# All three terms of a split float32 product summed in the same 256 PSUM columns, with another weight offset in each layer

## The chip, the cores and the metric

The kernel runs on one core of a Trainium2 chip. The metric is device time in microseconds (us) of one execution. Before the change it is 2197.75 us, the median of three runs (2196.8 to 2198.79).

## What is computed

The reference is a two-layer decoder trunk on 256 tokens of width 2048, in float32. Cut to what matters:

```python
for layer in range(2):
    hn = rms_norm(h, mix_norm_w[layer])
    mix = even_mixer(hn, ...) if layer % 2 == 0 else odd_mixer(hn, ...)
    h = h + mix
    f = conv_ffn(rms_norm(h, ffn_norm_w[layer]), ...)   # (silu(conv(hn @ w_gate)) * (hn @ w_up)) @ w_down
    h = h + f
return rms_norm(h, final_norm_w)
```

`even_mixer` is one wide input projection that feeds stick-breaking attention (8 heads) and a Mamba-2 state-space part, and an output projection. `odd_mixer` is dilated attention with 16 heads. The feed-forward width is 5632. Nearly all arithmetic is in the large matrix products, and all their weights are read once from device memory.

## The kernel before, in words

**Split products.** TensorE takes its operands as `float32r`. Each float32 operand is therefore kept as two parts, a rounded `hi` and the rest `lo`, and a product is the sum of three terms: w_hi·x_hi, w_hi·x_lo and w_lo·x_hi. An activation tile (`x`, `act` or `o`, 128 partitions x 512 columns) holds x_hi of the 256 tokens in its first half and x_lo in its second.

**Weights.** `prep` (L131) loads a chunk of 512 KB (128 x 1024) into a `raw` tile (4 buffers) with a DMA from SyncE's queue, ScalarE casts it into the hi part of an `hl` tile (3 buffers; L149), and VectorE subtracts to get the lo part (L150). In `hl` the hi part begins 48 elements into the tile and the lo part 1040 elements after it. In the built program every `x`, `act`, `o` and `hl` tile starts 64 bytes past a multiple of 128 bytes, so the distance from an activation tile to a weight part, taken modulo 128 bytes, is the part's offset in the tile times 4: 64 for hi, 0 for lo.

**Matmuls.** `chan` (L214) works off one chunk: weights stationary (128 x 128), tokens moving. For each of 2 output tiles and 4 slices k, a 512 wide matmul multiplies w_hi by x_hi and x_lo side by side into 512 PSUM columns, and a 256 wide one adds w_lo·x_hi to the first 256. So the sum of a product stands in two halves of a PSUM bank, and the eviction has to add them: `total` (L280) copies one half to SBUF on ScalarE (L284) and adds the other on VectorE (L285), and `project` (L376) adds both halves to the residual (L387, L388). A group of `chan` work has two PSUM banks out of the four of the `acc` pool. The opening (L161) does the first columns of the even layer with weights of its own layout: 16 tiles of `wfirst`, 816 columns each, of which `FB` = 304 belong to the first part; there six 272 wide matmuls (L186) with tokens stationary stand beside four pairs of 512 and 256 (L194, L196). `tok` (L226) does value projections with the roles turned: tokens stationary, weights moving, 512 wide (L231) and 256 wide (L238); its weights stand 48 elements into `hl` and it is not changed. `wide` (L413) does the last projections, 512 wide, L419.

**Order.** `products` (L245) walks over the chunks of a layer; background generators (attention, the state-space part, normalisation) give out a piece of their work per chunk. The engines' order is set when the program is built, by a scheduler that follows its own estimate of when operands are ready; each engine then works strictly in that order. The state-space part needs 32 rows of sums, which go to device memory (`rows`, L818, a DMA from ScalarE's queue) and come back broadcast to all partitions (`sr`, L823, four DMAs of 512 KB from GpSimd's queue). VectorE uses them at L875. Phases: even layer, feed-forward 0, odd layer, feed-forward 1.

Of the kernel before, what the change touches and what calls it, by code (L numbers as in the profile page):

```python
# [21 lines left out]
FT = FF // P  # L22
CH = 4

FB = 304
FW = FB + 2 * T
SBH = 8
SBW = 1024
# [36 lines left out]
class Trunk:  # L65
# [5 lines left out]
    def __init__(self, ctx, tc, a):  # L71
        self.tc = tc
        self.nc = tc.nc
        self.a = a
        pool = lambda name, bufs, **kw: ctx.enter_context(tc.tile_pool(name=name, bufs=bufs, **kw))
        self.cst = pool("cst", 1)
        self.hp = pool("hp", 1)
        self.xp = pool("xp", KT)
        self.wraw = pool("wraw", 4)
        self.whl = pool("whl", 3)  # L80
        self.dram = pool("dram", 1, space=bass.MemoryType.DRAM)
        self.ev = pool("ev", 3)
        self.nrm = pool("nrm", 2)
        pool("gap", 1).tile([P, 48], F32, name="gap")
        self.acc = pool("acc", 4, space=bass.MemoryType.PSUM)
        self.aux = pool("aux", 4, space=bass.MemoryType.PSUM)
        self.n = 0
        self.bg = []
        self.last = None
        self.strict = {}  # L90

    def nm(self, s):
        self.n += 1
# [37 lines left out]
    def prep(self, src, apart=False, off=48):  # L131


        nc = self.nc
        ch, ncol = src.shape[-2:]
        n = ch * ncol
        raw = self.wraw.tile([P, CH * 272], F32, tag="raw", name=self.nm("raw"))[:, :n]
        hl = self.whl.tile([P, CH * 544], F32R, tag="hl", name=self.nm("hl"))
        raw = raw.rearrange("p (c n) -> p c n", n=ncol)
        if apart:  # L140
            both = hl = tuple(
                hl[:, o : o + n].rearrange("p (c n) -> p c n", n=ncol) for o in (48, 48 + n + 16)
            )
        else:
            hl = hl[:, off : off + 2 * n].rearrange("p (c t n) -> p c t n", t=2, n=ncol)
            both = (hl[:, :, 0], hl[:, :, 1])
        nc.sync.dma_start(raw, src)
        hi, lo = both
        nc.scalar.copy(hi, raw)  # L149
        nc.vector.tensor_tensor(lo, raw, hi.bitcast(F32), ALU.subtract)  # L150
        return hl
# [9 lines left out]
    def opening(self, xs):  # L161


        nc = self.nc
        mm = nc.tensor.matmul
        accs = [self.banks(self.acc), self.banks(self.acc), self.banks(self.aux)]
        n = T + SSH
        lo0 = FW + 32
        for k in range(KT):
            raw = self.wraw.tile([P, CH * 272], F32, tag="raw", name=self.nm("raw"))  # L170
            hl = self.whl.tile([P, CH * 544], F32R, tag="hl", name=self.nm("hl"))
            parts = (slice(0, FB), slice(FB, FW)) if k == 0 else (slice(0, FW),)
            for s in parts:
                self.then(nc.sync, "dma_start", raw[:, s], self.a["wfirst"][k][:, s])
            xs.load(k + 1 + k // 4)
            for s in parts:
                hi, lo = hl[:, s], hl[:, lo0 + s.start : lo0 + s.stop]
                self.then(nc.scalar, "copy", hi, raw[:, s])
                self.then(nc.vector, "tensor_tensor", lo, raw[:, s], hi.bitcast(F32), ALU.subtract)
                if k == s.start == 0:  # L180
                    xs.split(0)
            xs.split(k + 1 + k // 4)
            x = xs[k]
            for p, w in ((0, 0), (0, lo0), (1, 0)):
                for tt in range(NT):
                    mm(  # L186
                        accs[0][tt][:, :n], x[:, p * T + tt * P : p * T + (tt + 1) * P], hl[:, w : w + n],
                        start=k == p == w == 0, stop=k == KT - 1 and p == 1,
                    )
            for j in (0, 1):  # L190
                for nt in range(2):
                    acc = accs[1 + j][nt]
                    c = FB + j * T + nt * P
                    mm(acc, hl[:, c : c + P], x, start=k == 0, stop=False)  # L194
                    c += lo0
                    mm(acc[:, :T], hl[:, c : c + P], x[:, :T], start=False, stop=k == KT - 1)  # L196
            if k == KT - 1:
                self.strict = None
            self.tick()
        return accs  # L200
# [13 lines left out]
    def chan(self, accs, hl, xs, k0, start, stop):  # L214


        for nt in range(2):
            for k in range(CH):
                for w in range(2):
                    n = (2 - w) * T  # L220
                    self.nc.tensor.matmul(  # L221
                        accs[nt][:, :n], hl[w][:, k, nt * P : (nt + 1) * P], xs[k0 + k][:, :n],
                        start=start and k == w == 0, stop=stop and w == 1 and k == CH - 1,
                    )

    def tok(self, accs, hl, xs, k0, start, stop):  # L226
# [47 lines left out]
    def tick(self):  # L274

        for g in list(self.bg):
            if next(g, self) is self:
                self.bg.remove(g)

    def total(self, acc):  # L280

        nc = self.nc
        t = self.ev.tile([P, T], F32, tag="ev", name=self.nm("ev"))
        nc.scalar.copy(t, acc[:, T:])  # L284
        nc.vector.tensor_tensor(t, acc[:, :T], t, ALU.add)  # L285
        return t

    def padded(self, n, count):

# [86 lines left out]
    def project(self, panels, xs, normw, order=None):  # L376

        nc = self.nc
        sums = []
        out = []  # L380

        def done(g):
            def f(accs):
                for nt, acc in enumerate(accs):
                    kt = 2 * g + nt
                    h = self.h[kt]
                    nc.vector.tensor_tensor(h, acc[:, T:], h, ALU.add)  # L387
                    nc.vector.tensor_tensor(h, acc[:, :T], h, ALU.add)  # L388
                    out.append(self.split_scaled(h, normw(kt)))
                self.square(sums, self.pair(2 * g))  # L390

            return f

        self.products([(self.chan, panels[g], done(g)) for g in range(KT // 2)], xs, order)
        return out, sums
# [96 lines left out]
    def ffn(self, l, xs, sums, normw, out=None):  # L492
# [10 lines left out]
        def gate(g):  # L503
            def f(accs):
                for nt, acc in enumerate(accs):
                    j = 2 * g + nt
                    gp = gpad[j % 3]
                    nc.vector.tensor_tensor(gp[:, 2:], self.total(acc), self.rbc, ALU.mult)  # L508
                    c = self.t256("cv", 4)
                    w = lambda i: self.par("fcw", (l * 3 + i) * FT + j)  # L510
                    nc.scalar.activation(c, gp[:, 2:], AF.Copy, scale=w(2))  # L511
                    nc.vector.scalar_tensor_tensor(c, gp[:, 1 : T + 1], w(1), c, ALU.mult, ALU.add)  # L512
                    nc.vector.scalar_tensor_tensor(c, gp[:, :T], w(0), c, ALU.mult, ALU.add)  # L513
                    self.last = nc.scalar.activation(c, c, AF.Silu, bias=self.par("fcb", l * FT + j))  # L514
                    nc.gpsimd.tensor_tensor(c, c, self.rbc, ALU.mult)  # L515
                    sil[j] = c

            return f

        def up(g):  # L520
            def f(accs):
                for nt, acc in enumerate(accs):
                    j = 2 * g + nt
                    u = self.total(acc)
                    nc.vector.tensor_tensor(u, u, sil.pop(j), ALU.mult)  # L525
                    self.split(u, act[j])

            return f
# [131 lines left out]
    def heads(self, panels, g, attend, o, v=None, vi=0):  # L660
# [9 lines left out]
        def qdone(accs):  # L670
            for acc in accs:
                t = self.t256("q")
                nc.vector.scalar_tensor_tensor(t, self.total(acc), ISD, self.rbc, ALU.mult, ALU.mult)
                q.append(t)

        def kdone(accs):
            for acc in accs:
                t = self.t256("k")
                nc.vector.tensor_tensor(t, self.total(acc), self.rbc, ALU.mult)
                k.append(t)  # L680
            self.bg.append(attend(q, k, v, o, vi))

# [25 lines left out]
    def even(self, xs, sums, normw):  # L708
# [21 lines left out]
        def convdone(g):  # L730

            def f(accs):
                pair = self.big("ssd", 14, F32)
                self.convs.append(pair)
                for nt, acc in enumerate(accs):
                    j = 2 * g + nt
                    cp = cpad[j % 2]
                    nc.vector.tensor_tensor(cp[:, 3:], self.total(acc), self.rbc, ALU.mult)
                    c = self.t256("cv", 3)
                    w = lambda i: self.par("ecw", i * 12 + j)  # L740
                    nc.scalar.activation(c, cp[:, 3:], AF.Copy, scale=w(3))
# [10 lines left out]
        def zdone(accs):  # L752
            pair = self.big("ssd", 14, F32)
            for nt, acc in enumerate(accs):
                c = self.total(acc)
                nc.vector.tensor_tensor(c, c, self.rbc, ALU.mult)
                dst = pair[:, nt * T : (nt + 1) * T]
                self.last = nc.scalar.activation(dst, c, AF.Silu)
                zs.append(dst)
# [152 lines left out]
    def run(self, out):  # L912
# [53 lines left out]

        xs = Input()
        ffnw = lambda l: lambda k: self.par("ffnw", l * KT + k)
        for step in (
            lambda x, s: self.even(x, s, ffnw(0)),  # L970
            lambda x, s: self.ffn(0, x, s, lambda k: self.par("mixw", KT + k)),
            lambda x, s: self.odd(x, s, ffnw(1)),
        ):
            with self.phase() as self.ph:
                xs, sums = step(xs, sums)
        with self.phase() as self.ph:
            self.ffn(1, xs, sums, None, out)


# [94 lines left out]
```

## Time and profile before

| | |
|---|---|
| median of the runs | 2197.75 us |
| the profiled execution, whole | 2196.1 us |
| its span, first to last instruction | 2194.0 us |
| TensorE busy | 2181.3 us, 12414 matmuls |
| TensorE weight loads | 1909.6 us, 12414 loads |
| VectorE busy | 1438.4 us |
| ScalarE busy | 1139.8 us |
| mean DMA rate | 190 GB/s |

In the rows of the profile PE is TensorE's matmul, PEld its weight load, DVE VectorE, ACT ScalarE, POOL GpSimd and SP SyncE. A matmul record is some 160 ns longer than the time to the next start, since matmuls are pipelined: how fast TensorE goes is read from the starts (or from the number that starts in a window), never from the mean length of a record.

### The profile page before, as it was taken

To read this page: it belongs to the slowest core of one execution; us is meant where nothing else is said; L and a number is where in the kernel's file an instruction comes from. 1 tells how busy PE (TensorE), PEld (TensorE's weight loads), DVE (VectorE), ACT (ScalarE), POOL (GpSimd) and SP (SyncE) were. 2 spreads that over 40 slices of the span, in tenths; PEclk is the share of its full clock that TensorE was granted. 3 is DMA by queue.
4 is the path that set the end of the run, shared out by engine and by line. 5 is a ranking of instruction groups with operands and counts; after the bars stand their busy time and mean duration, and the time that the engine had idled before them with its cause. 6 is when DMAs were issued, how large, how long until landed. Compare 5 with 4: busy or idle time off the path is not lost.

```text
span 2194.0 us, 32170 instructions
## 1 busy us (share of the span) xinstructions
PE 2181.3 (99%) x12414; PEld 1909.6 (87%) x12414; DVE 1438.4 (66%) x2096; ACT 1139.8 (52%) x1647; POOL 96.8 (4%) x107
## 2 busy tenths in 40 slices
PE   9999999999999999999999999999999999999998
PEld 8888888888888888888888888888888888888886
DVE  8678776766667665555566556667667676654444
ACT  7456554555555554444455454546555555554443
POOL 0000000111101010000000000000010101100000
PEclk9999999999999999999999999999999999999999
DMA  7754556666666666666655555566566666666664
GB/s 251 231 175 152 173 181 193 189 195 192 193 194 193 196 194 193 193 192 195 195 176 175 180 168 179 183 212 189 184 193 194 194 196 194 192 194 193 196 195 154
DMA packets 117129, 417.43 MB, mean 190 GB/s; under 512 B 13008, under 2 KB 15216, under 8 KB 116848
## 3 DMA queue, kind: packets, MB, share of 16 engines
q1 hardware_dynamic: 115776, 412.48, 61.0%
q8 instruction: 97, 1.59, 0.3%
q0 software_dynamic: 576, 2.10, 0.3%
q10 hardware_dynamic: 624, 0.81, 0.1%
q14 instruction: 56, 0.46, 0.1%
HBM read 413.22 MB, written 2.11 MB: 189 GB/s over the span
## 4 chain that ended last, share of the span: by engine, by line
PE 98%; DMA 1%; DVE 0%; ACT 0%; issue 0%; POOL 0%; DVEq 0%
PE acc L221 78%; PE acc L419 15%; PE acc L231 1%; PE acc L194 1%; PE acc L186 1%; DMA sr<-rows 1%; PE acc L238 1%; PE acc L196 0%; PE aux L613 0%; PE aux L644 0%; PE aux L635 0%; PE aux L890 0%; PE aux L159 0%; PE aux L552 0%; PE aux L596 0%; PE aux L645 0%
## 5 line engine op out<-in xcount | busy, mean ns | idle before, releaser
L150 DVE TENSOR_TENSOR hl<-raw,hl 128x1024 fp32r<-128x1024 f32 x764 | 935.0, 1224 | 676.2 <-ACT hl L149 669.3
L221 PE MATMUL acc<-x,hl 128*128 128x512 f32 (+1 forms) x7680 | 1320.5, 333 | 2.7 <-DVE hl L150 2.6
L221 PEld LDWEIGHTS acc<-x,hl 128*128 128x128 f32 x7680 | 1156.9, 188 | 153.9 <-DVE hl L150 4.0
L149 ACT CAST hl<-raw 128x1024 fp32r<-128x1024 f32 x764 | 802.1, 1050 | 834.6 <-PE acc L221 527.5
L419 PE MATMUL acc<-hl,act 128*128 128x512 f32 x1056 | 239.5, 389 | 0.0
L221 PE MATMUL acc<-act,hl 128*128 128x512 f32 (+1 forms) x1408 | 239.5, 332 | 0.0
L221 PEld LDWEIGHTS acc<-act,hl 128*128 128x128 f32 x1408 | 211.8, 188 | 27.6
L419 PEld LDWEIGHTS acc<-hl,act 128*128 128x128 f32 x1056 | 198.1, 188 | 41.1
L221 PE MATMUL acc<-o,hl 128*128 128x512 f32 (+1 forms) x1024 | 175.1, 333 | 0.0
L221 PEld LDWEIGHTS acc<-o,hl 128*128 128x128 f32 x1024 | 154.1, 188 | 20.1
L284 ACT COPY ev<-acc 128x256 f32<-128x256 f32 x244 | 90.6, 373 | 148.3 <-PE acc L221 146.3
L515 POOL TENSOR_TENSOR cv<-cv,rbc 128x256 f32<-128x256 f32 x88 | 93.7, 1083 | 860.3 <-ACT cv L514 860.3
L285 DVE TENSOR_TENSOR ev<-acc,ev 128x256 f32<-128x256 f32 x244 | 102.0, 420 | 5.0 <-ACT ev L284 3.1
L419 PE MATMUL acc<-hl,x 128*128 128x512 f32 x384 | 90.5, 393 | 0.0
L419 PEld LDWEIGHTS acc<-hl,x 128*128 128x128 f32 x384 | 71.5, 188 | 14.8
L525 DVE TENSOR_TENSOR ev<-ev,cv 128x256 f32<-128x256 f32 x88 | 38.3, 437 | 10.2 <-POOL cv L515 1.5
L292 POOL MEMSET pad<- 128x2 f32 (+1 forms) x8 | 0.5, 100 | 929.7 <-PE acc L221 929.7
L514 ACT ACTIVATE cv<-cv,params 128x256 f32<-128x256 f32 x88 | 40.0, 502 | 0.0
L511 ACT ACTIVATE cv<-pad,params 128x256 f32<-128x256 f32 x88 | 39.9, 504 | 0.0
L508 DVE TENSOR_TENSOR pad<-ev,rbc 128x256 f32<-128x256 f32 x88 | 37.5, 426 | 3.0
L512 DVE SCALAR_TENSOR_TENSOR cv<-pad,params,cv 128x256 f32<-128x256 f32 x88 | 38.4, 478 | 0.0
L513 DVE SCALAR_TENSOR_TENSOR cv<-pad,params,cv 128x256 f32<-128x256 f32 x88 | 38.4, 477 | 0.0
(187 smaller groups left out, 842.7 us busy)
## 6 DMA issues: line engine op xcount, KB each, us to landing
raw<-in_wg SPq DMA_DIRECT2D x176, 512.0 KB, 3.7
raw<-in_wu SPq DMA_DIRECT2D x176, 512.0 KB, 3.6
raw<-in_wd SPq DMA_DIRECT2D x176, 512.0 KB, 3.6
raw<-in_wev SPq DMA_DIRECT2D x76, 512.0 KB, 4.0
raw<-in_wod SPq DMA_DIRECT2D x64, 512.0 KB, 3.6
raw<-in_wevo SPq DMA_DIRECT2D x32, 512.0 KB, 4.1
raw<-in_wodv SPq DMA_DIRECT2D x32, 512.0 KB, 3.9
raw<-in_wodo SPq DMA_DIRECT2D x32, 512.0 KB, 3.5
```

The source lines that it names most:

```text
L149: nc.scalar.copy(hi, raw)
L150: nc.vector.tensor_tensor(lo, raw, hi.bitcast(F32), ALU.subtract)
L221: self.nc.tensor.matmul(accs[nt][:, :n], hl[w][:, k, nt * P : (nt + 1) * P], xs[k0 + k][:, :n], start=start and k == w == 0, stop=stop and ...
L284: nc.scalar.copy(t, acc[:, T:])
L285: nc.vector.tensor_tensor(t, acc[:, :T], t, ALU.add)
L419: self.nc.tensor.matmul(acc, part(xs[k0 + k], p), hl[:, k, w, :], start=start and n == k == 0, stop=stop and n == 2 and k == ch - 1,)
L511: nc.scalar.activation(c, gp[:, 2:], AF.Copy, scale=w(2))
L512: nc.vector.scalar_tensor_tensor(c, gp[:, 1 : T + 1], w(1), c, ALU.mult, ALU.add)
L513: nc.vector.scalar_tensor_tensor(c, gp[:, :T], w(0), c, ALU.mult, ALU.add)
L514: self.last = nc.scalar.activation(c, c, AF.Silu, bias=self.par("fcb", l * FT + j))
L515: nc.gpsimd.tensor_tensor(c, c, self.rbc, ALU.mult)
L525: nc.vector.tensor_tensor(u, u, sil.pop(j), ALU.mult)
```

## The change

All three terms go to the same 256 columns: `chan` and the opening issue three 256 wide matmuls (hi·x_hi, hi·x_lo, lo·x_hi) where there were one of 512 and one of 256. The halves are then not added any more: `total` is gone, its users read PSUM directly, and `project` adds once. The hi part of the weights begins at `self.dist` elements and the lo part right behind it; `dist` is 16 in the even layer, 20 in feed-forward 0, 24 in the odd layer and 12 in feed-forward 1, so the distance modulo 128 bytes is 64, 80, 96 and 48, the same for hi and lo. In the opening the first part of `wfirst` gets 32 more columns of zeros (816 to 848 columns in all), so that hi and lo both stand at 64.

```diff
-FB = 304
+FB = 272 + 64
...
-                hl[:, o : o + n].rearrange("p (c n) -> p c n", n=ncol) for o in (48, 48 + n + 16)
+                hl[:, o : o + n].rearrange("p (c n) -> p c n", n=ncol) for o in (self.dist, self.dist + n)
...
-        lo0 = FW + 32
+        lo0 = FW + 48
...
-                    acc = accs[1 + j][nt]
+                    acc = accs[1 + j][nt][:, :T]
                     c = FB + j * T + nt * P
-                    mm(acc, hl[:, c : c + P], x, start=k == 0, stop=False)
-                    c += lo0
-                    mm(acc[:, :T], hl[:, c : c + P], x[:, :T], start=False, stop=k == KT - 1)
+                    for w, p in ((0, 0), (0, 1), (lo0, 0)):
+                        mm(
+                            acc, hl[:, c + w : c + w + P], x[:, p * T : (p + 1) * T],
+                            start=k == w == p == 0, stop=w > 0 and k == KT - 1,
+                        )
...
     def chan(self, accs, hl, xs, k0, start, stop):
+        terms = ((0, 0), (0, 1), (1, 0))
         for nt in range(2):
             for k in range(CH):
-                for w in range(2):
-                    n = (2 - w) * T
+                for n, (w, p) in enumerate(terms):
                     self.nc.tensor.matmul(
-                        accs[nt][:, :n], hl[w][:, k, nt * P : (nt + 1) * P], xs[k0 + k][:, :n],
-                        start=start and k == w == 0, stop=stop and w == 1 and k == CH - 1,
+                        accs[nt][:, :T], hl[w][:, k, nt * P : (nt + 1) * P], xs[k0 + k][:, p * T : (p + 1) * T],
+                        start=start and k == n == 0, stop=stop and n == 2 and k == CH - 1,
                     )
...
-                    nc.vector.tensor_tensor(h, acc[:, T:], h, ALU.add)
                     nc.vector.tensor_tensor(h, acc[:, :T], h, ALU.add)
...
-                    nc.vector.tensor_tensor(gp[:, 2:], self.total(acc), self.rbc, ALU.mult)
+                    nc.vector.tensor_tensor(gp[:, 2:], acc[:, :T], self.rbc, ALU.mult)
...
-        for step in (
+        for dist, step in zip((16, 20, 24, 12), (
...
+                self.dist = dist
                 xs, sums = step(xs, sums)
         with self.phase() as self.ph:
+            self.dist = 12
             self.ffn(1, xs, sums, None, out)
```

The other users of `total` (the up half of the feed-forward, q, k, the convolution and the gate of the state-space part) change as the gate of the feed-forward does.

On TensorE, the first chunk behind the opening begins like this before (`acc` is the PSUM bank, `x` the tokens, `hl` the weights; the last field is partitions x columns):

```order
L221 MATMUL acc_572<-x_151,hl_575 128x512
L221 MATMUL acc_572<-x_151,hl_575 128x256
L221 MATMUL acc_572<-x_156,hl_575 128x512
L221 MATMUL acc_572<-x_156,hl_575 128x256
L221 MATMUL acc_572<-x_181,hl_575 128x512
L221 MATMUL acc_572<-x_181,hl_575 128x256
```

The same place after the change:

```order
L224 MATMUL acc_636<-x_151,hl_639 128x256 x3
L224 MATMUL acc_636<-x_156,hl_639 128x256 x3
L224 MATMUL acc_636<-x_185,hl_639 128x256 x3
L224 MATMUL acc_636<-x_212,hl_639 128x256 x3
L224 MATMUL acc_637<-x_151,hl_639 128x256 x3
```

Every pair has become three of one width; the columns that move stay 768 for each slice.

The scheduler also moved the small matmuls that make the 32 rows (`s` are the sums). On TensorE before, they stand inside the fifth chunk behind the opening (`hl_739`), with four transposes of the state-space part right behind them:

```order
L221 MATMUL acc_573<-x_462,hl_705 128x256
L221 MATMUL acc_736<-x_151,hl_739 128x512
L221 MATMUL acc_737<-x_151,hl_739 128x512
L808 MATMUL aux_908<-s_617,consts 128x32
L809 MATMUL aux_908<-s_617,consts 128x16
L811 MATMUL aux_911<-consts,s_617 32x128
L837 MATMUL aux_1375<-consts,ssd_641 128x128 x2
L837 MATMUL aux_1375<-consts,ssd_683 128x128 x2
L221 MATMUL acc_736<-x_151,hl_739 128x256
```

After the change they stand behind the eleventh chunk:

```order
L224 MATMUL acc_950<-x_396,hl_1010 128x256 x3
L802 MATMUL aux_1038<-s_689,consts 128x32
L803 MATMUL aux_1038<-s_689,consts 128x16
L805 MATMUL aux_1041<-consts,s_689 32x128
L224 MATMUL acc_949<-x_426,hl_1056 128x256 x3
L224 MATMUL acc_949<-x_453,hl_1056 128x256 x3
```

They come seven chunks later, and the four transposes are no longer with them.

On VectorE before, the first use of the broadcast rows (`ex<-sr`) stands behind the subtract of the eighth chunk, and the lo parts of later chunks stand behind it (`cv`, `pad` and `ev` belong to the convolution):

```order
L150 TENSOR_TENSOR hl_802<-raw_801,hl_802 128x1024
L875 TENSOR_SCALAR ex_1513<-sr_920,s_913 128x128 x2
L150 TENSOR_TENSOR hl_846<-raw_845,hl_846 128x1024
L875 TENSOR_SCALAR ex_1513<-sr_920,s_913 128x128 x2
L150 TENSOR_TENSOR hl_867<-raw_866,hl_867 128x1024
L285 TENSOR_TENSOR ev_823<-acc_736,ev_823 128x256
L738 TENSOR_TENSOR pad_135<-ev_823,rbc_545 128x256
```

After the change it stands behind the subtract of the fifteenth:

```order
L151 TENSOR_TENSOR hl_1152<-raw_1151,hl_1152 128x1024
L869 TENSOR_SCALAR ex_1781<-sr_1050,s_1043 128x128 x2
L151 TENSOR_TENSOR hl_1181<-raw_1180,hl_1181 128x1024
L151 TENSOR_TENSOR hl_1227<-raw_1226,hl_1227 128x1024
L869 TENSOR_SCALAR ex_1781<-sr_1050,s_1043 128x128 x2
L151 TENSOR_TENSOR hl_1256<-raw_1255,hl_1256 128x1024
```

The wait for the rows has moved seven chunks down, and the second wait now has two subtracts ahead of it instead of one.

More of the change, by code (lines that the diff above doesn't have):

```diff
@@ L90, in __init__ @@
         self.strict = {}
+        self.dist = 16
     def nm(self, s):
@@ L278, in tick @@
                 self.bg.remove(g)
[L280 to L286, printed above, removed]
     def padded(self, n, count):
@@ L523, in f @@
                     j = 2 * g + nt
-                    u = self.total(acc)
-                    nc.vector.tensor_tensor(u, u, sil.pop(j), ALU.mult)
+                    u = self.ev.tile([P, T], F32, tag="ev", name=self.nm("ev"))
+                    nc.vector.tensor_tensor(u, acc[:, :T], sil.pop(j), ALU.mult)
                     self.split(u, act[j])
@@ L672, in qdone @@
                 t = self.t256("q")
-                nc.vector.scalar_tensor_tensor(t, self.total(acc), ISD, self.rbc, ALU.mult, ALU.mult)
+                nc.vector.scalar_tensor_tensor(t, acc[:, :T], ISD, self.rbc, ALU.mult, ALU.mult)
                 q.append(t)
@@ L678, in kdone @@
                 t = self.t256("k")
-                nc.vector.tensor_tensor(t, self.total(acc), self.rbc, ALU.mult)
+                nc.vector.tensor_tensor(t, acc[:, :T], self.rbc, ALU.mult)
                 k.append(t)
@@ L737, in f @@
                     cp = cpad[j % 2]
-                    nc.vector.tensor_tensor(cp[:, 3:], self.total(acc), self.rbc, ALU.mult)
+                    nc.vector.tensor_tensor(cp[:, 3:], acc[:, :T], self.rbc, ALU.mult)
                     c = self.t256("cv", 3)
@@ L754, in zdone @@
             for nt, acc in enumerate(accs):
-                c = self.total(acc)
-                nc.vector.tensor_tensor(c, c, self.rbc, ALU.mult)
+                c = self.ev.tile([P, T], F32, tag="ev", name=self.nm("ev"))
+                nc.vector.tensor_tensor(c, acc[:, :T], self.rbc, ALU.mult)
                 dst = pair[:, nt * T : (nt + 1) * T]
@@ L968, in run @@
         ffnw = lambda l: lambda k: self.par("ffnw", l * KT + k)
-        for step in (
+        for dist, step in zip((16, 20, 24), (
             lambda x, s: self.even(x, s, ffnw(0)),
@@ L972, in run @@
             lambda x, s: self.odd(x, s, ffnw(1)),
-        ):
+        )):
             with self.phase() as self.ph:
+                self.dist = dist
                 xs, sums = step(xs, sums)
         with self.phase() as self.ph:
+            self.dist = 12
             self.ffn(1, xs, sums, None, out)
```

## The prediction

> **What bounds the kernel now.** I read the page's busy times first, then the chain that ended last, then who waits for whom.
>
> ```profile
> span 2194.0 us, 32170 instructions
> PE 2181.3 (99%) x12414; PEld 1909.6 (87%) x12414; DVE 1438.4 (66%) x2096; ACT 1139.8 (52%) x1647; POOL 96.8 (4%) x107
> ...
> PE 98%; DMA 1%; DVE 0%; ACT 0%; issue 0%; POOL 0%; DVEq 0%
> ...
> PE acc L221 <- DVE hl L150: 2.6, 3, 1.9
> PEld acc L221 <- DVE hl L150: 4.0, 5, 2.2
> ```
>
> TensorE is 98% of the chain, and its matmuls wait for VectorE 2.6 us in all, its weight loads 4.0 us, largely the same moments. So nothing that VectorE or ScalarE saves is worth more than some 4 us; everything else is TensorE's pace. A busy share of 99% doesn't say how good that pace is, since the records overlap. I count starts: in long windows at granted clock 1.00 (number of matmuls in brackets), and in the chain's two longest unbroken pieces (start, length, count).
>
> ```profile
> 600.00:700.00 100.00, 100.00 (x589) 1.00 0.63 194
> 1700.00:1800.00 100.00, 100.00 (x589) 1.00 0.63 194
> 2000.00:2100.00 100.00, 100.00 (x443) 1.00 0.64 192
> ...
> 382.02 712.66 PE acc L221 x4192
> ...
> 1946.15 239.40 PE acc L419 x1056
> ```
>
> The piece from 382 us holds nothing but pairs of 512 and 256: 712.5 us without the last record's overhang for 2096 pairs, **340 ns a pair**. The piece from 1946 us is 512 wide alone: 239.2 / 1056 = **226.6 ns each**. A 256 wide matmul beside it thus takes 340 - 226.6 = **113.4 ns**, half of that to a tenth of a nanosecond. The time goes with the moving columns, and no fixed cost of a start is seen.
>
> **What the change makes of TensorE's work.** The number of slices that change:
>
> ```profile
> L221 PE MATMUL acc<-x,hl 128*128 128x512 f32 x3840 | 1313.1, 390 | 0.0
> L221 PE MATMUL acc<-act,hl 128*128 128x512 f32 x704 | 239.4, 389 | 0.0
> L221 PE MATMUL acc<-o,hl 128*128 128x512 f32 x512 | 174.6, 389 | 0.0
> L194 PE MATMUL acc<-x,hl 128*128 128x512 f32 x64 | 22.2, 390 | 0.0
> ```
>
> These are 3840 + 704 + 512 + 64 = **5120 slices**, each with one pair now and three 256 wide matmuls after. By columns: 3 x 113.3 = 340 ns against 340, so 0 for all of them.
>
> What hides the third weight load? Before, a load runs beside each matmul: lo beside the 512 wide one, with time to spare, and the next hi beside the 256 wide one, in 113 ns. After, all three run beside 256 wide ones, 5120 loads more and none with spare time. Does a row of 256 wide matmuls, each with its own load, hold the pace? `tok` has runs of four (starts in the first column):
>
> ```profile
> 189.70 1.09 PE L231 MATMUL acc<-hl,x 128*128 128x512 f32 x4
> 190.63 0.62 PE L238 MATMUL acc<-hl,x 128*128 128x256 f32 x4
> 191.08 0.39 PE L231 MATMUL acc<-hl,x 128*128 128x512 f32 x1
> ...
> 193.32 0.64 PE L238 MATMUL acc<-hl,x 128*128 128x256 f32 x4
> 193.79 1.10 PE L231 MATMUL acc<-hl,x 128*128 128x512 f32 x4
> ```
>
> The first run takes 191.08 - 190.63 = 0.45 us, 113 ns each; the second 0.47 us, 117.5 ns each. Both are at a distance of 64 bytes modulo 128. The four 512 wide ones between take 0.93 us, 232 each, not 226. So distance and history do move the pace, by 4 to 6 ns a matmul. The opening shows a third case, tokens stationary, 272 wide:
>
> ```profile
> 24.56 0.91 PE L186 MATMUL acc<-hl,x 128*128 128x272 f32 x6
> 25.31 0.39 PE L194 MATMUL acc<-x,hl 128*128 128x512 f32 x1
> ```
>
> 0.75 us for six, 125 ns each, where the columns alone give 272/256 x 113.3 = 120.4.
>
> **The distances** are the unknown cost. The even layer's 64 has its row, the 113 ns run. For 80, 96 and 48 there is none: every part of `hl` stands at a multiple of 64 bytes before. Bounds from the nearest rows: 113.3 ns at best, the pace of every undisturbed window; 117.5 for the slow run of four; 125 x 256/272 = 117.6 for the opening's. Nothing excludes a gain, which I bound by as much again below. I take 113.3: 48 and 80 stand 16 bytes from a distance with a good row, 96 stands 32.
>
> [...]
>
> **What VectorE and ScalarE lose.**
>
> ```profile
> L284 ACT COPY ev<-acc 128x256 f32<-128x256 f32 x244 | 90.6, 373 | 148.3 <-PE acc L221 146.3 <-DVE ev L285 2.0
> L285 DVE TENSOR_TENSOR ev<-acc,ev 128x256 f32<-128x256 f32 x244 | 102.0, 420 | 5.0 <-ACT ev L284 3.1
> L387 DVE TENSOR_TENSOR h<-acc,h 128x256 f32<-128x256 f32 x48 | 19.7, 416 | 0.0
> ```
>
> ScalarE loses 244 copies, 91 us, VectorE 292 additions, 122 us. Behind a TensorE that waits under 4 us this is worth nothing by itself. The banks are given back about 0.8 us sooner (0.37 + 0.42), but a group lasts 4 chunks x 8 x 0.34 = 10.9 us on the other two banks, so nobody waited for them.
>
> **The places where TensorE waits.** All of it is near the broadcast rows:
>
> ```profile
> 51.93 0.30 PE L808 MATMUL aux<-s,consts 128*128 128x32 f32 x2
> ...
> 53.74 0.33 PE L837 MATMUL aux<-consts,ssd 128*128 128x128 f32 x1 [0.48 <-ACT ssd L745]
> 54.32 14.11 PE L221 MATMUL acc<-x,hl 128*128 128x256 f32 x79 [0.25 <-DVE hl L150]
> 70.31 5.78 PE L221 MATMUL acc<-x,hl 128*128 128x256 f32 x32 [1.87 <-DVE hl L150]
> 76.54 3.69 PE L221 MATMUL acc<-x,hl 128*128 128x256 f32 x20 [0.46 <-DVE hl L150]
> ...
> 63.68 0.49 DVE L875 TENSOR_SCALAR ex<-sr,s 128x128 f32<-128x128 f32 x2 [4.45 <-DMA sr<-rows]
> 64.08 1.22 DVE L150 TENSOR_TENSOR hl<-raw,hl 128x1024 fp32r<-128x1024 f32 x1
> 68.64 0.48 DVE L875 TENSOR_SCALAR ex<-sr,s 128x128 f32<-128x128 f32 x2 [3.34 <-DMA sr<-rows]
> 69.04 1.22 DVE L150 TENSOR_TENSOR hl<-raw,hl 128x1024 fp32r<-128x1024 f32 x1
> ```
>
> VectorE waits in order for the rows, and the lo parts that TensorE needs stand behind that wait: 0.25 + 1.87 + 0.46 = 2.6 us lost, and 0.48 for a transpose. The rows come 11.8 and 16.7 us after L808. After the change their matmuls stand behind the eleventh chunk. The opening ends at 40.4; a chunk is 8 x 0.34 = 2.72; so they start at 40.4 + 11 x 2.72 = 70.3, and the rows come at 82.1 and 87.0. The sixteenth chunk, behind the first wait, is due at 70.3 + 0.8 + 4 x 2.72 = 82.0, and its subtract ends at 82.1 + 0.4 + 1.2 = 83.7: **TensorE waits 1.7**. The eighteenth is due at 83.7 + 5.4 = 89.1, and its subtract ends at 87.0 + 1.6 = 88.6: no wait. So 1.7 in place of 2.6, and the 0.48 is gone: -1.4 us. POOL's four row DMAs are the same in number and only later; SP's weight loads keep their order.
>
> The opening's first part grows from 304 to 336 columns:
>
> ```profile
> 3.37 0.44 ACT L119 CAST hl<-raw 128x304 fp32r<-128x304 f32 x1 [0.42 <-DMA raw<-in_wfirst]
> 3.85 0.47 DVE L116 TENSOR_TENSOR hl<-raw,hl 128x304 fp32r<-128x304 f32 x1 [2.85 <-ACT hl L119]
> ```
>
> A tenth more of 0.44 and 0.47 and of the load ahead is 0.1 to 0.2 us before the first product. The 15 other loads grow by 4%; TensorE runs through from 12 us on, so its work covers them.
>
> **The sum:** 0 - 1.4 + 0.2 = -1.2 us on the profiled execution's 2196.1, 2194.9. The median of the runs is 1.65 above that execution, so **2196.5 us**.
>
> **The rivals.**
> (1) *The pace doesn't hold*: with no 512 wide matmul left to catch up beside, the streams stay at the slow spacing, 117.5 ns. Price: 4.2 x 3 = 12.6 ns a slice, 64 us if it holds for all 5120, 2261 us. For feed-forward 0 and 1 alone (48 and 80; 2112 + 1408 slices) 44 us, 2241; for the odd layer alone (768) 10 us. It decides from 0.3 ns a matmul on. For it: six matmuls of 272 in a row are always slow, and three of the four distances are unseen. Against: the runs of four reach 113. Chance **0.40**.
> (2) *TensorE's sequencer becomes the bound*: three slices' matmuls and loads are 6 instructions in 340 ns, 57 ns each, and the long piece shows only 4, 85 each. The opening's 125 ns for a load and a matmul would be 62.5 an instruction; then a slice is 375 ns, 179 us more, 2376. Against: the run of four at 113 ns. [...] Chance **0.05**.
> (3) *Faster*: a distance at which the load doesn't meet the moving stream lets 256 columns go below 113 ns. With 2 ns a matmul: 31 us less, 2166. No row is below the common pace, whatever the layout. Chance **0.10**.
> (4) Forecast: **0.45**, of which 0.04 with all waits gone and past the bound for faster.
>
> That the change doesn't do what it says (a second load of the same weights left out, say) would alter no time here, as the columns set the pace.
>
> **How the numbers follow.** What a measurement can tell from no change is about 0.2%, 4.4 us. Faster: 0.10 + 0.04 = 0.14. Same: 0.41 of the forecast and 0.02 of rival 1, where one small layer is a little slow: 0.43. Slower: 0.38 + 0.05 = 0.43. The range runs from 2191, the forecast with every wait gone, to 2261, rival 1 in full; rivals 2 and 3 are left out. The forecast's own range is 2192 to 2201.
>
> **What would show it.** The 100 us windows at 600 and 1700 should hold some 883 matmuls; 850 would be rival 1, 800 rival 2, over 890 rival 3, and the four phases differ if the distance decides. The wait for `sr` should stand near 82 and 87 us, with one TensorE wait of 1 to 2 us behind it. The prediction is wrong if the windows differ by over 1% from 883.

## The result, and the profile after

The changed kernel takes 2259.03 us, the median of four runs (2258.64 to 2260.65), beside 2197.28 us for the kernel before (four runs, 2196.31 to 2198.79). The ratio is 1.0282, with a 95% interval of 1.0264 to 1.03: 62 us slower. The profiled execution took 2258.64 us.

The page of the changed kernel, its span, busy times, chain by engine and the waits of TensorE:

```profile
span 2256.9 us, 41845 instructions
PE 2247.0 (100%) x17534; PEld 2177.9 (97%) x17534; DVE 1358.8 (60%) x1804; ACT 1064.6 (47%) x1403; POOL 97.4 (4%) x107
...
PE 99%; DMA 0%; DVE 0%; ACT 0%; issue 0%; DVEq 0%; ACTq 0%
...
PE acc L224 <- DVE hl L151: 0.3, 1, 0.3
PEld acc L224 <- DVE hl L151: 0.5, 1, 0.5
```

VectorE and ScalarE have lost their evictions (80 and 75 us less busy), TensorE waits less than before, and the span is 62.9 us longer. So the time is in TensorE's pace. The windows of the changed kernel, TensorE alone (window, busy time, matmuls that start in it, granted clock, share of the DMA engines, GB/s):

```profile
300.00:340.00 40.00, 40.00 (x355) 1.00 0.58 190
600.00:700.00 100.00, 100.00 (x844) 1.00 0.56 185
1700.00:1800.00 100.00, 100.00 (x851) 1.00 0.56 186
```

At 113.3 ns a window of 100 us holds 883 matmuls and one of 40 us 353. The even layer holds that pace in this window; feed-forward 0 (600) starts one every 118.5 ns, feed-forward 1 (1700) one every 117.5. The clock is 1.00 in all three, and the weights move more slowly than before (194 GB/s in the windows of before), so neither the clock nor the memory is what ends last.

The long unbroken pieces of the chain give each phase to a tenth of a nanosecond (start, length, matmuls). In the changed kernel:

```profile
286.67 87.46 PE acc L224 x768
...
380.76 746.84 PE acc L224 x6288
...
1418.60 96.77 PE acc L224 x816
...
1627.42 381.61 PE acc L224 x3240
2009.02 239.42 PE acc L413 x1056
```

In the kernel before, the pieces at the same places of the even layer, the odd layer and feed-forward 1:

```profile
288.60 87.06 PE acc L221 x512
...
1378.44 92.50 PE acc L221 x544
...
1578.93 367.23 PE acc L221 x2160
```

Divided by the matmuls, the changed kernel has 113.9 ns at 64 bytes (even), 118.8 at 80 (feed-forward 0), 118.6 at 96 (odd) and 117.8 at 48 (feed-forward 1). In this and the kernels below the pieces of the even and the odd layer run on for some 9 us into the feed-forward behind them; up to 365.41 us, where feed-forward 0 begins, the even layer here has 113.4. The 512 wide stretch at the end, which the change does not touch, takes 239.4 us in both. From the first product of a phase to that of the next, feed-forward 0 grew from 719.0 to 753.6 us (16.4 ns for each of its 2112 slices), the odd layer from 376.3 to 387.7 (14.9 ns for each of 768) and feed-forward 1 from 483.4 to 502.1 (13.3 ns for each of 1408). The opening and the even layer together fell from 367.3 to 365.4, with their waits. The sum is 62.9 us, which is what the span grew by.

### The profile page after: what moved, and what is told of

Read it like the earlier page. It is cut to its first block, busy times and chain, and to the rows that moved or that the text cites. A ratio compares the mean times of both kernels' runs of the same rounds, so it can differ in the third digit from the quotient of the medians.

```text
span 2256.9 us, 41845 instructions
## 1 busy us (share of the span) xinstructions
PE 2247.0 (100%) x17534; PEld 2177.9 (97%) x17534; DVE 1358.8 (60%) x1804; ACT 1064.6 (47%) x1403; POOL 97.4 (4%) x107
## 4 chain that ended last, share of the span: by engine, by line
PE 99%; DMA 0%; DVE 0%; ACT 0%; issue 0%; DVEq 0%; ACTq 0%
PE acc L224 79%; PE acc L413 14%; PE acc L196 1%; PE acc L234 1%; PE acc L187 1%; PE acc L241 0%; PE aux L607 0%; PE aux L638 0%; DMA sr<-rows 0%; PE aux L629 0%; PE aux L884 0%; PE aux L590 0%; PE aux L546 0%; PE aux L160 0%; PE aux L606 0%; PE aux L639 0%
## 5 line engine op out<-in xcount | busy, mean ns | idle before, releaser
L224 PE MATMUL acc<-x,hl 128*128 128x256 f32 x11520 | 1370.2, 281 | 0.3 <-DVE hl L151 0.3
L224 PEld LDWEIGHTS acc<-x,hl 128*128 128x128 f32 x11520 | 1361.5, 188 | 2.1 <-issue 0.9
L224 PE MATMUL acc<-act,hl 128*128 128x256 f32 x2112 | 251.0, 282 | 0.0
L224 PEld LDWEIGHTS acc<-act,hl 128*128 128x128 f32 x2112 | 251.0, 189 | 0.0
L224 PE MATMUL acc<-o,hl 128*128 128x256 f32 x1536 | 179.5, 279 | 0.0
L224 PEld LDWEIGHTS acc<-o,hl 128*128 128x128 f32 x1536 | 179.0, 188 | 0.1
L364 ACT CAST act<-ev 128x256 fp32r<-128x256 f32 x88 | 35.5, 404 | 69.2 <-DVE ev L519 69.2
L506 DVE SCALAR_TENSOR_TENSOR cv<-pad,params,cv 128x256 f32<-128x256 f32 x88 | 62.8, 713 | 0.7
L507 DVE SCALAR_TENSOR_TENSOR cv<-pad,params,cv 128x256 f32<-128x256 f32 x88 | 42.7, 485 | 3.1
L519 DVE TENSOR_TENSOR ev<-acc,cv 128x256 f32<-128x256 f32 x88 | 37.1, 421 | 11.1 <-PE acc L224 9.4
L502 DVE TENSOR_TENSOR pad<-acc,rbc 128x256 f32<-128x256 f32 x88 | 37.1, 422 | 8.6 <-PE acc L224 8.6
```

Source lines behind the costliest of these rows:

```text
L224: self.nc.tensor.matmul(accs[nt][:, :T], hl[w][:, k, nt * P : (nt + 1) * P], xs[k0 + k][:, p * T : (p + 1) * T], start=start and k == n == ...
L364: nc.scalar.copy(hi, src)
L502: nc.vector.tensor_tensor(gp[:, 2:], acc[:, :T], self.rbc, ALU.mult)
L519: nc.vector.tensor_tensor(u, acc[:, :T], sil.pop(j), ALU.mult)
```

## The experiments

Two theories stood at first: that the distance between the moving tokens and the next weights, modulo 128 bytes, sets the pace (D), and that a stream of 256 wide matmuls cannot hold it once there is no 512 wide one beside them (N). Later ones are named as they come. No kernel here leaves out or changes a part of the computation; they place its operands at other addresses or add spare work. Where one time is given, it is of one execution.

### One distance, 64 bytes, in every layer

```diff
-        for dist, step in zip((16, 20, 24), (
+        for dist, step in zip((16, 16, 16), (
...
-            self.dist = 12
+            self.dist = 16
```

> The changed kernel with dist = 16 in all four phases, so weights and tokens are 64 bytes apart modulo 128 everywhere. Theory D (the distance sets the pace): the 100 us windows at 600 and 1700 hold some 882 matmuls instead of 844 and 851 (340 ns a slice), and the time is 2195 us, within 4 us of the kernel before. Theory N (the third start or weight load of a slice costs 4 ns a matmul whatever the distance): the windows stay near 845 and the time stays near 2259 us.

Measured: 2212.22 us (2211.12 to 2212.27), 1.0067 times the kernel before, 95% interval 1.0053 to 1.0081. Its windows and the long pieces of its chain:

```profile
600.00:700.00 100.00, 100.00 (x885) 1.00 0.60 195
1700.00:1800.00 100.00, 100.00 (x851) 1.00 0.57 187
```

```profile
381.15 712.66 PE acc L224 x6288
...
1379.56 92.50 PE acc L224 x816
...
1581.01 381.60 PE acc L224 x3240
```

Feed-forward 0 and the odd layer's long stretch are back at 113.3 ns, to a hundredth of a microsecond what the pairs took before. So N falls: 256 wide matmuls hold the pace for 712 us. But feed-forward 1, at the same distance, stays at 117.8 from 1581 us to its end. In its earlier part, four transposes (left out below) interrupt the stream every 11 us, and the pieces between them alternate:

```profile
1500.82 10.90 PE acc L224 x96
...
1512.16 11.31 PE acc L224 x96
...
1523.90 10.90 PE acc L224 x96
...
1535.24 10.90 PE acc L224 x96
...
1546.58 11.31 PE acc L224 x96
...
1558.33 10.90 PE acc L224 x96
...
1569.67 10.90 PE acc L224 x96
```

10.90 us is 113.5 ns a matmul, 11.31 is 117.8. At 64 bytes there are two paces, and an interruption can change from one to the other.

### Other distances

A rival to D was that the weights' own alignment decides (A): in the kernel before, every weight part stands at a multiple of 64 bytes. Three kernels took four distances each, in the order even, feed-forward 0, odd, feed-forward 1, with the same two lines edited: `dist` 16, 0, 8, 48 (64, 0, 32 and 192 bytes, the last the same as 64 modulo 128).

> The changed kernel with dist 16, 0, 8 and 48: distances modulo 128 of 64 in the even layer, 0 in feed-forward 0, 32 in the odd layer, 64 (192 bytes) in feed-forward 1. Theory D, with a period of 128 bytes: feed-forward 1 goes at 340 ns a slice, feed-forward 0 at 355 or more, the odd layer's tokens at 350 or more; some 2240 us. Theory A (what counts is that the weights start at a multiple of 64 bytes): feed-forward 0 goes at 340 too, only the odd layer is slow, some 2205 us. Theory N: all slow, 2259 us.

Measured: 2252.26 us.

```profile
383.80 754.42 PE acc L224 x6288
...
1429.21 96.52 PE acc L224 x816
...
1635.47 367.21 PE acc L224 x3240
```

0 bytes is the worst so far, 120.0 ns, though its weights are aligned to 64 bytes; 32 bytes takes 118.3; 192 bytes runs at 113.3 in its long stretch, behind pieces at 117.8. A falls.

Then `dist` 14, 15, 18, 17: 56, 60, 72 and 68 bytes, to see how wide the good place is.

> The changed kernel with dist 14, 15, 18, 17: 56 bytes in the even layer, 60 in feed-forward 0, 72 in the odd layer, 68 in feed-forward 1. If a band around 64 bytes is good: 60 and 68 reach 113.3 ns a matmul at least in some stretches, 56 and 72 perhaps. If only 64 itself is good: all stay at 117 to 119 ns, as 48 and 80 did; some 2260 us.

Measured: 2273.19 us.

```profile
291.83 90.59 PE acc L224 x768
...
389.05 751.25 PE acc L224 x6288
...
1431.28 96.56 PE acc L224 x816
...
1640.18 383.40 PE acc L224 x3240
```

56 bytes takes 118.0 ns, 60 takes 119.5, 72 and 68 take 118.3. A single float32 away from 64 the pace is lost in every stretch that was run.

Then `dist` 28, 4, 6, 30: 112, 16, 24 and 120 bytes.

> The changed kernel with dist 28, 4, 6, 30: 112 bytes in the even layer, 16 in feed-forward 0, 24 in the odd layer, 120 in feed-forward 1. If the cost grows with the way from 64: all at 118.5 to 120 ns, between 48 or 80 (117.8, 118.8) and 0 (120.0); some 2270 us. If another good distance exists in the range, its phase goes at 113.3 ns.

Measured: 2277.83 us, the slowest of all. The same pieces take 92.03 us (112 bytes, 119.8 ns), 744.11 (16 bytes, 118.3), 96.89 (24 bytes, 118.7) and 386.84 (120 bytes, 119.4). Of the fifteen distances tried in these kernels and the changed one, only 64 and 192, which are the same modulo 128, ever hold 113.3 ns. None is faster, and the cost does not fall steadily towards 64. Each of the other thirteen was met in one phase of one kernel only, those of feed-forward 0 (0, 16, 60 and 80) nearly all in one unbroken stretch. Since 64 and 192 have slow stretches too, and the end of feed-forward 1 takes 381.61 us at 48 bytes beside 381.60 in the slow stretch at 64, it is not shown that the others can never be fast.

### The distance kept, the addresses moved

All distances 64, and an unused tile of 32 bytes ahead of the pools, so that tokens and weights all stand 32 bytes further on. TensorE's instructions stand in the same order as with 64 bytes everywhere; so they do in every kernel here that has three narrow matmuls, up to the interruptions added below.

```diff
+        pool("shift", 1).tile([P, 8], F32, name="shift")
```

> As dist = 16 in all phases, with every token and weight tile moved up by 32 bytes: the distance stays 64, but weights and tokens no longer start at a multiple of 64 bytes. Theory D: 340 ns a slice, about 2195 us, windows of some 882. Theory A: slow in all phases, 118 ns a matmul, windows of some 845 and 2260 us.

Measured: 2197.18 us, with every long piece at 113.3 ns.

```profile
380.24 712.66 PE acc L225 x6288
...
1580.36 367.22 PE acc L225 x3240
```

No operand of these matmuls is aligned to 64 bytes now and the pace is full, so A falls again. But feed-forward 1, slow for its last 381.60 us without the shift, is fast with it, at the same distance and in the same order. To see whether that is chance of one execution, the same kernel was timed:

> The kernel of e3_shift32 again (64 bytes everywhere, all tiles 32 bytes up), timed. If the steady spacing is picked by the order and timing of the program and not by chance in each execution, all executions are near 2197 us and feed-forward 1 goes at 340 ns a slice again; the ratio to before is 1.000 within 0.002. If it is drawn anew in each execution, some are near 2212 us.

Measured: 2197.25 us over 11 runs (2196.69 to 2200.12), 1.0003 times the kernel before, 95% interval 0.9994 to 1.0011. The repeat ran on another chip, and in both profiled executions every stretch of 60 or more matmuls has the same pace: here the paces of the long stretches went with the built program. About 290 of its 5120 slices still take 351 to 356 ns, in short stretches of the even and odd layers.

Not every stretch repeats. The even layer is at 64 bytes, with the same instructions in the same order, in the changed kernel, in the one with 64 everywhere, in the first sweep and in the kernel of the next section. Its first stretch in the first two of them:

```profile
40.83 30.20 PE acc L224 x264
```

```profile
41.18 31.34 PE acc L224 x264
```

The first sweep took 31.35 us for it, the kernel of the next section 30.19. Between one execution and another, the same instructions at the same distance went at either pace; a difference of 1.2 us is too small to stand out in the times of the runs.

### Interruptions added

Is the pace chosen where the stream restarts (H), or is it fixed by the place in the program (P)? Distances of 64 everywhere, no shift, and in feed-forward 1 twelve more interruptions, each two small matmuls into a spare bank.

```diff
+    def interrupt(self):
+        for _ in range(60):
+            yield
+        for _ in range(12):
+            ps = self.psum()
+            for _ in range(2):
+                self.nc.tensor.matmul(ps[:, :P], self.ones, self.ident, start=True, stop=True)
+            for _ in range(8):
+                yield
```

> The kernel with 64 bytes everywhere (e1_all64), whose last phase ran at 353 ns a slice from its last interruption at 1580 us to 1962 us, with 12 extra interruptions: two 128 wide float32 matmuls into a spare bank, every eighth chunk from the sixtieth of feed-forward 1 on. They change no distance. Theory H (at 64 bytes there are two steady spacings, 113.3 and 117.8 ns, and the phase in which the stream restarts behind an interruption picks one): stretches of some 22 us between the interruptions, some at 113.3 and some at 117.8 ns. Theory P (something of this phase itself, its tiles or its other work, holds it slow): 117.8 in all of them. Some 12 x 0.4 us for the interruptions come on top.

Measured: 2216.41 us. The pieces between the first added interruptions:

```profile
1637.66 22.62 PE acc L224 x192
...
1660.73 21.78 PE acc L224 x192
...
1682.95 22.62 PE acc L224 x192
...
1706.01 22.62 PE acc L224 x192
```

One of the eleven pieces between the added interruptions goes at 113.4 ns, the rest at 117.8. The stretch that was slow without a break in the first experiment thus turns fast and slow again by being interrupted. That is for H, but with one fast piece behind a dozen restarts it says little of how the choice is made.

### What the 512 wide matmul did before

The kernel before holds 340 ns a slice with its lo weights at 0, where narrow matmuls alone took 120.0 ns. One reason could be that only the load beside the narrow matmul counts, which there is the next hi part at 64, while the lo part at 0 loads beside the wide one. So in the kernel before, with its pairs, the parts were moved: hi 80 and lo 0 in feed-forward 0, hi 64 and lo 16 in the odd layer, both at 64 in feed-forward 1, nothing changed in the even layer.

```diff
-                hl[:, o : o + n].rearrange("p (c n) -> p c n", n=ncol) for o in (48, 48 + n + 16)
+                hl[:, o : o + n].rearrange("p (c n) -> p c n", n=ncol) for o in self.places
...
-        for step in (
+        for places, step in zip(((48, 1088), (52, 1088), (48, 1092)), (
...
+            self.places = (16, 1040)
```

> The kernel before (pairs of 512 and 256), with hi and lo parts placed per phase: unchanged in the even layer; feed-forward 0 with hi at 80 and lo at 0 bytes modulo 128; odd layer with hi at 64 and lo at 16; feed-forward 1 with both at 64. If the distance only makes the weight load longer (theory L): the hi load stands beside the 256 wide matmul, which becomes 118 to 119 ns, so feed-forward 0 takes 345 to 346 ns a slice; the lo load beside the 512 wide one is hidden, so the odd layer and feed-forward 1 stay at 340: 2207 us. If the moving stream itself is slowed by a bad distance (theory S): odd layer and feed-forward 1 too, 345 to 350 ns a slice, and the time is 2225 us or more.

Measured: 2233.9 us.

```profile
384.58 726.80 PE acc L222 x4192
...
1397.69 92.83 PE acc L222 x544
...
1602.33 381.60 PE acc L222 x2160
```

With hi at 80 a pair takes 346.7 ns, most of the cost in the narrow matmul (118.8 ns, the wide one 228.0). With lo at 16 the longest stretch of the odd layer holds 341, but four others, of 64 to 80 matmuls, go at 353, which none of them does in the kernel before. With both at 64 a pair takes 353.3 throughout feed-forward 1, and there a 512 wide matmul takes 235.0 ns from start to start in place of 226.6. So the load beside the narrow matmul is not all that decides, and the wide one is not safe either.

Nor are the old places always fast. In the kernel before, all 24 stretches of 60 or more matmuls settle at 340 ns a pair. But the even layer, where this run changes nothing, has a slow one. Here it is, and below it the stretch at that place in the kernel before:

```profile
70.27 57.59 PE acc L222 x319
```

```profile
76.54 49.02 PE acc L221 x287
```

In the run, TensorE's granted clock stood at 0.50 from 72 to 74 us, behind a wait of 1.94 us; then, at clock 1.00, the pairs went at 350 ns (118 and 232) up to the next interruption, some 53 us. In the kernel before, the clock stayed at 1.00 there, and the pairs were back at 340 within a few slices of each wait.

And the change without its new places: three 256 wide matmuls, with hi at 64 and lo at 0 as before.

```diff
-                hl[:, o : o + n].rearrange("p (c n) -> p c n", n=ncol) for o in (self.dist, self.dist + n)
+                hl[:, o : o + n].rearrange("p (c n) -> p c n", n=ncol) for o in (48, 48 + n + 16)
```

> One part of the change alone: three 256 wide matmuls a slice, with the places of before (hi at 64, lo at 0 bytes modulo 128; the opening as in the change). If each load costs by its own distance: two matmuls at 113.3 and the one beside the lo load at 120, 347 ns a slice, some 2230 us. If one bad load of three spoils the whole slice: 353 to 360 ns, 2260 to 2295 us. If places don't matter as long as a good load follows: 340 ns, 2197 us.

Measured: 2259.68 us, as slow as the whole change.

```profile
389.62 740.59 PE acc L224 x6288
...
1628.46 381.61 PE acc L224 x3240
```

A slice takes 353.3 ns on average in every phase, and no stretch is fast. Of its three loads two are at 64 and one at 0. If each paid for itself, the slice would take 113.3 + 113.3 + 120.0 = 346.6. In the long piece of feed-forward 0 its three starts stand 120, 118.3 and 115 ns apart instead, over and over: the cost is not that of one matmul alone. The sum is that of the slow pace at 64, but the pattern is not, as there all starts are 117 to 119 ns apart. Beside the kernel before, which has the same places and the pairs, this run shows that the split costs some 62 us without any new place.

### One distance of 192 bytes

> The changed kernel with dist = 48 in all phases, 192 bytes, 64 modulo 128. Theory H: every long stretch goes either at 113.3 or at 117.8 ns a matmul, none between, and the time is between 2196 us (all fast) and 2260 us (all slow), depending on where the long stretches restart. If the period of the distance is 256 bytes and not 128, other spacings appear.

`dist` 48 in every layer. Measured: 2238.57 us (2238.07 to 2240.11), 1.0189 times the kernel before, 95% interval 1.0174 to 1.0205.

```profile
290.84 87.05 PE acc L224 x768
...
384.43 740.59 PE acc L224 x6288
...
1621.60 367.21 PE acc L224 x3240
```

The same distance modulo 128 as 64, with the phases the other way round: feed-forward 0 is slow for 740.59 us, where it was fast for 712.66, and the end of feed-forward 1 is fast, where it was slow. Every stretch of 90 or more matmuls goes at 113.3 or at 117.8 ns, none between. So a good distance allows the fast pace and does not secure it.

## Why the prediction was wrong

**What bounds the kernel** was right: TensorE is 99% of the chain after, and the evictions that VectorE and ScalarE lost brought nothing by themselves. They were fewer microseconds than counted on, 80 and 75 in place of 122 and 91, as some of the operations that stay have longer records (L506, in the convolution, 713 ns on average in place of 478).

**The pace** is the step that failed: "I take 113.3: 48 and 80 stand 16 bytes from a distance with a good row, 96 stands 32". The sum had 0 for 5120 slices; the trace has some 65 us. The reading took the pace for a smooth function of the distance. Of the fifteen distances only 64 and 192 were ever fast, and 4 bytes beside 64 the cost was whole. The working had the unknown where it was, and both of its ends, 113.3 and 117.5, turned out to be, within 0.3 ns, the two paces of a stream at 64 bytes. What was misread is the pair of runs of four at L238: 0.45 and 0.47 us, at one distance, were those two paces side by side. They were taken as a good row and a bad one; they said that even a good distance does not fix the pace. The kernel before has 24 such runs: 19 start at 118 ns and go on at 113 to 114, four go at 117.8 throughout, and one lies between. These last five, and no others, stand right behind an interruption.

**Rival 1** is what happened, at the time it gave: 2261 against 2259.03. Its mechanism, streams that stay at the slow spacing with no 512 wide matmul beside them, is right with a condition that it lacked: at 64 bytes the stream was fast for as long as 712 us. And the wide matmul is no sure remedy, as pairs were slow too (353 ns with both parts at 64, 350 once at the old places). Its total is partly luck: it charged all 5120 slices 12.6 ns, while the even layer, at 64, paid little (some 130 of its 768 slices took 351 to 356 ns) and the phases at 80 and 96 paid 16.4 and 14.9 ns a slice.

**Rival 2**, the sequencer, falls: with 64 bytes, six instructions every 340 ns (57 ns each) are kept up for 712 us. **Rival 3**, a faster distance, falls as far as it was looked for: none of the fifteen distances goes below 113.3.

**A fixed cost of a start**, of which the prediction saw none, does not show after the split either: with 64 bytes, three starts in 340.0 ns take what two took before, to within 0.01 us in 712.66.

**The waits.** The chosen step had the rows at 82.1 and 87.0 us, and one wait of TensorE of 1.7. The timeline of the changed kernel (start, busy time, instruction, and in brackets the idle time before it and what ended it):

```profile
70.86 0.30 PE L802 MATMUL aux<-s,consts 128*128 128x32 f32 x2
...
81.70 0.48 DVE L869 TENSOR_SCALAR ex<-sr,s 128x128 f32<-128x128 f32 x2 [4.71 <-DMA sr<-rows]
82.09 2.36 DVE L151 TENSOR_TENSOR hl<-raw,hl 128x1024 fp32r<-128x1024 f32 x2
...
83.37 11.85 PE L224 MATMUL acc<-x,hl 128*128 128x256 f32 x102 [0.34 <-DVE hl L151]
85.39 0.48 DVE L869 TENSOR_SCALAR ex<-sr,s 128x128 f32<-128x128 f32 x2 [0.94 <-DMA sr<-rows]
```

The row sums start at 70.86 (70.3 was predicted), the rows come at 81.70 and 85.39, and TensorE waits 0.34 us behind the first, nowhere behind the second. The order of events was right; the wait was smaller, since the lo part was ready at 83.3 (82.09 and half of 2.36), not at 83.7, and TensorE came to it at 83.0 (83.37 less 0.34), not at 82.0. The gain, 2.3 us in place of 0.9, is lost in the rest. The opening's growth, put at 0.1 to 0.2 us before the first product, did not show there (4.44 us after, 4.49 before), but the opening ended at 40.81 in place of 40.38.

**What stays open.** Why, of the distances tried, only 64 bytes (and 192) had the fast pace was not found; that the two reads of TensorE, tokens and next weights, meet somewhere is the author's guess, and no run shows it. What the runs show is that the pace moves with the distance between them, by up to 6.7 ns in 113.3 (120.0 at 0 bytes). Which of the two paces a restart takes was not found either: for the long stretches of the shifted kernel it was the same in both profiled executions, while the first stretch of the even layer took 30.2 us in two kernels and 31.3 in two others; the pace changed with a shift of all addresses by 32 bytes, and at some interruptions. No version was found that beats both kernels; the shifted one with 64 bytes equals the kernel before.

## What to carry to other kernels

When a kernel is bound by TensorE's pace, read that pace from the starts, phase by phase, and treat the byte distance between the moving tile and the next weights as part of the design: at equal columns the distances, with a shift of all tiles by 32 bytes, moved this kernel by up to 3.7% (2277.83 us at the worst places, 2197.25 at the best). A row at one distance says little of a distance 4 bytes away (113.3 ns at 64 bytes, 119.5 at 60, 118.3 at 68), and two short runs at the same distance that differed by 4% (0.45 and 0.47 us) were two paces here, not noise. Splitting a wide matmul into narrow ones cost nothing by its columns (712.66 us for 2096 slices either way), but it lost a stability that the wide ones gave (353.3 ns a slice at the old places, where the pairs had 340), and the work taken from engines that nobody waits for, 80 and 75 us of it, paid for none of that.

## What was not expected of the hardware

A stream of 256 wide `float32r` matmuls at a distance of 64 bytes modulo 128 has two steady paces, not a spread: every start 113 or 114 ns behind the one before, or every start 117 to 119. Each holds for hundreds of microseconds (712.66 or 740.59 us for the same 6288 matmuls), and the long stretches of the shifted kernel kept theirs in both profiled executions. At other distances the starts scatter: at 80 bytes nearly all of them lie 115 to 121 ns apart, at 96 bytes 115 to 122, and at 60 bytes 115 to 133, 119.5 on average. Among the pairs of 512 and 256, with the lo part at 64 in place of 0, the distance at which narrow matmuls did best, the 512 wide matmul took 235.0 ns in place of 226.6 through all of feed-forward 1; that is one execution of one kernel.
